# Where the first gate pair's weights are made, and in which order the products of two gate pairs run, in a hybrid attention layer

## The chip, the cores and the metric

The kernel runs on one core of one Trainium2 chip. The metric is the device time of one execution in microseconds (us). A core has five engines that work through lists of their own, each in order: TensorE (PE in the profile; PEld are its weight loads), VectorE (DVE), ScalarE (ACT), GpSimd (POOL) and SyncE (SP), whose list is here the list of DMA transfers. They wait for one another by semaphores.

## The reference

One decoder layer on 2048 tokens of width 1024: a normalised input times one combined projection, two kinds of attention, two gated branches, a merge under two sigmoid gates, an output projection and a last norm.

```python
xn = rms_norm(h, norm_gain[l])
proj = xn @ w_in[l]
sb_q, sb_k, sb_v, sw_q, sw_k, sw_v, sb_z, sw_z, g_sb, g_sw = jnp.split(proj, offsets, axis=-1)
o_sb = stick_breaking_attention(...)
...
o_sw = sliding_window_sink_attention(q, k, ...)
y_sb = (o_sb * jax.nn.silu(sb_z)) @ w_branch_sb[l]
y_sw = (o_sw * jax.nn.silu(sw_z)) @ w_branch_swa[l]
merged = jax.nn.sigmoid(g_sb) * y_sb + jax.nn.sigmoid(g_sw) * y_sw
h = h + merged @ w_out[l]
```

The columns `sb_z`, `sw_z`, `g_sb` and `g_sw` of the projection are the gates. They need nothing of the attention, so their products can stand anywhere; the change is about them.

## The kernel before

**Tiling.** Tokens are cut in four groups of 512 (`GT`), columns of the projection in tiles of 128, the inner dimension in 8 slices of 128 (`KT`). Two halves, groups 2 and 3 first (half 0), then 0 and 1 (half 1), each go through projections, sliding-window attention, stick-breaking attention and gates. Every number is split in a high and a low part, and a product of two slices is three matmuls of 128x512: high by high, high by low, low by high (L415 to L417 in `gemm`, L688 in `seven`). A column tile of one group is 24 matmuls, of both groups 48.

**Weights.** `load` (L162) fetches a raw tile of 512 KB into a ring of two buffers, `raw`. `weights` (L167) splits it: ScalarE casts the high part `wh` (L109), VectorE subtracts for the low part `wl` (L112); `wh` and `wl` are rings of three buffers each. Half 0 writes both parts to DRAM (`kept`), and half 1 loads them from there. A buffer of a ring is given out in the order of the source and becomes free when its last reader is done.

**Gate tiles alone.** `gts` are the gate tiles. In each half `gts[1]` and `gts[2]` run alone ahead of the stick-breaking stage, `gts[3:rest]` (`REST` is 12 and 18) are woven between its rows, and two more follow it.

**Gate pairs.** From `gts[rest+2]` to `gts[25]` (14 to 25 in half 0, 20 to 25 in half 1) two tiles are taken together (`gate_pair`, L721): a 2x2 block product of two tiles by two groups in seven products instead of eight (`seven`, L682), each of 4 slices, 12 matmuls. The weight operands are called `11`, `12` (tile `a`, one ring buffer `t1`), `s2`, `s3` (buffer `t3`), `s1`, `22` (buffer `t2`) and `s4`; those of the tokens `11`, `21`, `t1` to `t4`. `pair_weights` (L631) makes the weight operands on ScalarE and VectorE from the raw tiles `a` and `b`: `t1` is `a` itself, the others are sums and differences of halves of both (L656 to L661), which overwrite a part of `b`. The first pair of half 0 is made early, ahead of the stick-breaking stage, and goes to DRAM as `p0` to `p3`, each with a high and a low part. A pair that is `plain` also stores `b` as it was, for which half of it is split first, in a `tmp` called `t5`. The other five pairs of half 0 are made where they are used; the first two of these are plain like the early one, the last three also go to DRAM as `p0` to `p3`, and are the three pairs of half 1, which loads them.

**What sets the order.** TensorE's order is that of the source, by hand (`manual_schedule`). In these stages the orders of ScalarE, VectorE and SP are decided by a scheduler. `in_line` (L738) steps through the pairs: the first pair's products `11` and `12·21` (it is the `lead`), then `s2·t2`, `s1·t1`, `s3·t3`, `22·t4`, then the next pair's weights and its `11`, then the first pair's last product `s4·22`; a pair that isn't the lead has `12·21` behind `s2·t2`. `u2` and `u3` are sums out of a PSUM bank that the next product writes again (L703, L710), `use` applies the gate function and the sums of other branches and stores.

Of the kernel before, what the change touches and what calls it, by code (L numbers as in the profile page):

```python
# [17 lines left out]
P = 128  # L18
# [24 lines left out]
def f32(ap):  # L43
    return ap.bitcast(F32)
# [3 lines left out]
def tile_kernel(ctx, tc, x, xt, meta, metat, gain, w_in, w_sb, w_sw, w_out, sinks, fgain,  # L48
# [579 lines left out]
            parted("t4", k, b21)  # L628
        yield q

    def pair_weights(bp, ca, cb, plain, early=False):  # L631

        t1, t3, t2 = ([wp.tile([P, KT, P], F32R, tag=t, name=t, bufs=3) for t in ("wh", "wl")] for _ in range(3))
        if early:
            t4 = [tmp(F32R).rearrange("p (k c) -> p k c", k=KT // 2) for _ in range(2)]
        else:
            t4 = [bp.tile([P, KT // 2, P], F32R, tag=t, name=t, bufs=2) for t in ("s4h", "s4l")]
        key = w_in.name, ca, cb
        if key in kept:
            for ts, ks in zip((t1, t3, t2, t4), kept[key]):  # L640
                for t, k in zip(ts, ks):
                    DMA(t, k)
        else:
            a, b = load(ca), load(cb)
            s = tp.tile([P, KT, P], F32, tag="vt", name="s", bufs=1)
            s4 = tmp().rearrange("p (k c) -> p k c", k=KT // 2)
            lo, hi = slice(0, KT // 2), slice(KT // 2, KT)

            def parts(hl, t):
                A.copy(hl[0], t)  # L650
                V.tensor_tensor(hl[1], t, f32(hl[0]), op=ALU.subtract)
            parts(t1, a)
            if plain:
                t5 = [tmp(F32R).rearrange("p (k c) -> p k c", k=KT // 2) for _ in range(2)]
                parts(t5, b[:, lo])
            V.tensor_tensor(s[:, hi], a[:, lo], b[:, lo], op=ALU.subtract)  # L656
            V.tensor_tensor(b[:, lo], b[:, lo], b[:, hi], op=ALU.add)
            V.tensor_tensor(s[:, lo], b[:, lo], a[:, lo], op=ALU.subtract)
            parts(t3, s)
            parts(t2, b)  # L660
            V.tensor_tensor(s4, a[:, hi], s[:, lo], op=ALU.subtract)  # L661
            parts(t4, s4)
            if plain:
                for c in (ca, cb):
                    kept[w_in.name, c] = [dram(f"{e}_{w_in.name}_{c}", [P, KT, P], F32R) for e in "hl"]
                for k, t in zip(kept[w_in.name, ca], t1):
                    DMA(k, t)
                for k, t, u in zip(kept[w_in.name, cb], t5, t2):
                    DMA(k[:, lo], t)
                    DMA(k[:, hi], u[:, hi])  # L670
            if early or not plain:
                kept[key] = []
                for n, ts in enumerate((t1, t3, t2, t4)):
                    kept[key].append([dram(f"p{n}{e}_{ca}", list(t.shape), F32R) for e, t in zip("hl", ts)])
                    for k, t in zip(kept[key][n], ts):
                        DMA(k, t)
        (t1h, t1l), (t3h, t3l), (t2h, t2l) = t1, t3, t2
        lo, hi = slice(0, KT // 2), slice(KT // 2, KT)
        return {"11": (t1h[:, lo], t1l[:, lo]), "12": (t1h[:, hi], t1l[:, hi]), "s2": (t3h[:, lo], t3l[:, lo]),
                "s3": (t3h[:, hi], t3l[:, hi]), "s1": (t2h[:, lo], t2l[:, lo]), "22": (t2h[:, hi], t2l[:, hi]), "s4": t4}  # L680

    def seven(w, b, tag, use, lead):  # L682

        def product(acc, n, m, first, last):
            (wh, wl), (bh, bl) = w[n], b[m]
            for k in range(KT // 2):
                for i, (l, r) in enumerate(((wh, bh), (wh, bl), (wl, bh))):
                    T.matmul(acc, lhsT=l[:, k, :], rhs=r[:, k, :], start=first and k == i == 0,  # L688
                             stop=k == KT // 2 - 1 and i == 2, skip_group_check=not (first and last))
        a0, p1 = ps("g"), tmp()  # L690
        product(a0, "11", "11", True, lead)
        A.copy(p1, a0)
        if lead:
            a3 = ps(tag)
            product(a3, "12", "21", True, True)
            t = tmp()
            V.tensor_tensor(t, a3, p1, op=ALU.add)
            use(0, 0, t)
        yield
        a1, a2 = ps("z"), ps("t")  # L700
        u2, u3 = tmp(), tmp()
        product(a1, "s2", "t2", True, False)
        V.tensor_tensor(u2, a1, p1, op=ALU.add)  # L703
        if not lead:
            product(a0, "12", "21", False, True)
            use(0, 0, a0)
        a3 = ps(tag)
        product(a2, "s1", "t1", True, False)
        product(a1, "s3", "t3", False, True)
        V.tensor_tensor(u3, a1, p1, op=ALU.add)  # L710
        product(a3, "22", "t4", True, True)
        V.tensor_tensor(p1, a2, u3, op=ALU.add)
        V.tensor_tensor(u3, a3, u3, op=ALU.add)
        use(1, 1, p1)
        use(1, 0, u3)
        yield
        product(a2, "s4", "22", False, True)
        V.tensor_tensor(u2, a2, u2, op=ALU.add)
        use(0, 1, u2)

    def gate_pair(bp, ga, gb, groups, q, tag, plain, lead, times):  # L721
        tiles = ga, gb

        def use(m, n, t):
            c0, dst, silu, src = tiles[m]
            e = tmp()
            A.activation(e, t, AF.Sigmoid)
            if silu:
                V.tensor_tensor(e, t, e, op=ALU.mult)
            if times:  # L730
                o = ring_x()
                DMA(o, src[groups[n]])
                V.tensor_tensor(e, e, o, op=ALU.mult)
            DMA(dst[groups[n]], e)
        w = pair_weights(bp, ga[0], gb[0], plain)
        yield
        yield from seven(w, q, tag, use, lead)

    def in_line(pairs):

        for n, g in enumerate(pairs):
            if n == 0:
                next(g)
                yield n
                next(g)
            next(g)
            if n + 1 < len(pairs):
                next(pairs[n + 1])
                next(pairs[n + 1])
            drain(g)  # L750
            yield n

# [553 lines left out]
    for half, groups in enumerate(halves):  # L1306
# [42 lines left out]
        with tc.tile_pool(name=f"sb{half}", bufs=1, side="left") as bp:  # L1349
            hsplit[0] = vsplit[0] = True  # L1350
            next_sums = {g: sums() for g in halves[1]} if half == 0 else {}
            side = stick(groups, bp, [(x[g * GT + i * P:g * GT + (i + 1) * P, f * GT:(f + 1) * GT], ssq[:, f, i:i + 1])
                                      for g, ssq in next_sums.items() for i in range(4) for f in range(2)])
            drain(tiles_by_tile(gts[1:2], groups))
            rest = REST[half]
            if half == 0:
                pair_weights(None, gss[0][rest + 2][0], gss[0][rest + 3][0], True, True)
            drain(tiles_by_tile(gts[2:3], groups))
            cost_sb = 8 * sum(4 * (4 - g) for g in groups) * 1.31 + 8 * 0.75
            ratio = cost_sb / ((rest - 3) * 10.4)  # L1360
            weave(tiles_by_tile(gts[3:rest], groups), side, ratio)
            drain(side)
        with tc.tile_pool(name=f"pairs{half}", bufs=1, side="left") as bp:
            ts = [mk() for mk in gts[rest:rest + 2]]
            sums_q = sums_of_x(bp, groups)
            tq = next(sums_q)
            for n, (w, use, _) in enumerate(ts):
                for i, g in enumerate(groups):
                    drain(lagged(col_tile(w, g, use, bank="gz"[i])))
            order = gss[half]  # L1370
            todo = in_line([gate_pair(bp, order[n], order[n + 1], groups, tq, ("o", "zm")[n // 2 % 2],
                                      half == 0 and n < PLAIN, n == rest + 2, half == 0) for n in range(rest + 2, 26, 2)])
            next(todo)
            next(sums_q)
            for n in todo:
                if half == 0 and n == 4:
                    t, u = (tmp()[:, :8] for _ in range(2))
                    for n, ssq in enumerate(next_sums.values()):
                        V.tensor_tensor(t[:, 4 * n:4 * n + 4], ssq[:, 0], ssq[:, 1], op=ALU.add)
                    rs = tp.tile([P, 8], F32, tag="rs8", name="rs", bufs=1)  # L1380
                    rsqrt(rs, t, tp, t=u)
                    rs0, rs1 = rs[:, :4], rs[:, 4:]
# [71 lines left out]
```

## Time and profile before

| what | us |
|---|---|
| three runs, median | 2141.4 |
| lowest and highest of the three | 2139.36 and 2141.83 |
| the profiled execution itself | 2139.68 |
| span of the profiled execution | 2138.0 |
| TensorE busy in it | 2091.8 |
| VectorE busy | 1497.1 |
| ScalarE busy | 1079.3 |
| mean granted clock of TensorE | 0.995 |

Times in profile rows count from the start of the span. A row of the timeline gives start, length, engine, line, operation and its tiles (buffer numbers left out), and in brackets how long the engine stood idle before it and what ended that. The gate tiles alone stand in half 0 around 371 us, its pairs from 637.6 us on, the pairs of half 1 from 1612 us on.

### The profile page before, as it was taken

The numbers are of one execution on the slowest core, as the hardware profiler recorded it, in microseconds if no ns is written. First come the engines' busy times: TensorE is split into PE (matmuls) and PEld (weight loads), VectorE is DVE, ScalarE is ACT, GpSimd is POOL, SyncE is SP. The second block draws the span as 40 slices with busy tenths as digits, with TensorE's granted clock in tenths as the row PEclk, the third lists the DMA queues.
The fourth block names the chain that finished last, engine by engine and source line by source line (L and its number), as shares of the span: only waits on it lengthen the run. The fifth ranks groups of instructions, "written<-read, shape, count | busy, mean of one in ns | idle before, by whom it ended". The sixth has DMA issues, their size and how long they took to land.

```text
span 2138.0 us, 29936 instructions
## 1 busy us (share of the span) xinstructions
PE 2091.8 (98%) x10426; PEld 1736.9 (81%) x10426; DVE 1497.1 (70%) x2389; ACT 1079.3 (50%) x2442; POOL 184.1 (9%) x373
## 2 busy tenths in 40 slices
PE   8999999899998999999999999999999999999998
PEld 7788887678877888888888888888888888887887
DVE  7897885578887863777756888989996336554453
ACT  6677774566643343677754656656552312221121
POOL 2122331000000000122210000000000000000000
PEclk9999999899999999999999999999999999999999
DMA  9855544975446985444446333333226786558532
GB/s 340 301 169 191 180 166 171 348 226 176 151 147 214 339 306 177 152 147 146 154 159 186 116 107 119 124 119 108 81 89 217 263 322 197 191 204 284 156 111 79
DMA packets 181142, 397.16 MB, mean 186 GB/s; under 512 B 23456, under 2 KB 41696, under 8 KB 180992
## 3 DMA queue, kind: packets, MB, share of 16 engines
q1 hardware_dynamic: 180992, 395.26, 54.5%
q8 instruction: 82, 1.34, 0.3%
q14 instruction: 68, 0.56, 0.1%
HBM read 245.74 MB, written 149.37 MB: 185 GB/s over the span
## 4 chain that ended last, share of the span: by engine, by line
PE 82%; DVE 8%; DMA 5%; ACT 3%; issue 2%; SPq 1%; DVEq 0%; ACTq 0%
PE ps_g L415 11%; PE ps_g L417 11%; PE ps_g L416 11%; PE ps_o L1106 5%; PE ps_t L1075 5%; PE ps_z L1050 5%; PE ps_o L934 3%; PE ps_z L888 2%; PE ps_z L688 2%; PE ps_t L688 2%; PE ps_g L688 2%; PE ps_g L237 1%; PE ps_g L238 1%; PE ps_g L236 1%; PE ps_z L238 1%
## 5 line engine op out<-in xcount | busy, mean ns | idle before, releaser
L415 PE MATMUL ps_g<-xh,wh 128*128 128x512 f32 x1224 | 503.2, 411 | 19.1 <-ACT wh L109 12.3
L416 PE MATMUL ps_g<-xl,wh 128*128 128x512 f32 x1224 | 481.4, 393 | 0.0
L417 PE MATMUL ps_g<-xh,wl 128*128 128x512 f32 x1224 | 481.2, 393 | 0.0
L415 PEld LDWEIGHTS ps_g<-xh,wh 128*128 128x128 f32 x1224 | 231.8, 189 | 56.1 <-ACT wh L109 12.7
L417 PEld LDWEIGHTS ps_g<-xh,wl 128*128 128x128 f32 x1224 | 230.7, 188 | 52.6 <-DVE wl L112 0.8
L416 PEld LDWEIGHTS ps_g<-xl,wh 128*128 128x128 f32 x1224 | 232.2, 190 | 36.0 <-DVE xl L1159 1.3
L1053 ACT ACTIVATE row<-ps_z 128x512 f32<-128x512 f32 (+2 forms) x320 | 165.4, 518 | 180.0 <-PE ps_z L1050 176.5
L1062 DVE TENSOR_TENSOR_SCAN row<-row 128x528 f32<-128x528 f32 (+1 forms) x192 | 210.6, 1097 | 19.8 <-ACT row L1053 15.4
L116 DVE SCALAR_TENSOR_TENSOR wtl<-ps_t,wth 128x512 fp32r<-128x512 f32 (+1 forms) x320 | 189.7, 593 | 18.5 <-ACT wth L115 17.8
L115 ACT ACTIVATE wth<-ps_t 128x512 fp32r<-128x512 f32 (+1 forms) x320 | 170.6, 533 | 58.3 <-PE ps_t L1075 56.0
L1060 DVE TENSOR_TENSOR_SCAN row<-row,mask 128x512 f32<-128x512 f32 (+4 forms) x128 | 144.2, 1131 | 69.1 <-ACT row L1053 68.0
L1050 PE MATMUL ps_z<-kt,q 128*128 128x512 f32 (+4 forms) x640 | 178.9, 355 | 0.0
L1075 PE MATMUL ps_t<-ident,row 128*128 128x128 f32 x1088 | 171.9, 273 | 6.3 <-DVE wtl L116 3.8
L1075 PEld LDWEIGHTS ps_t<-ident,row 128*128 128x128 f32 x1088 | 134.4, 140 | 41.1 <-DVE wtl L116 6.7
L1050 PEld LDWEIGHTS ps_z<-kt,q 128*128 128x128 f32 x640 | 117.4, 188 | 22.1 <-ACT row L1053 0.4
L1106 PE MATMUL ps_o<-wth,vc 128*128 128x512 f32 (+1 forms) x320 | 130.7, 409 | 1.0 <-ACT tmp L1110 0.9
L896 ACT ACTIVATE sc<-sc,nm 128x129 f32<-128x129 f32 x256 | 100.0, 393 | 40.9 <-DVE nm L894 40.2
L1106 PE MATMUL ps_o<-wtl,vc 128*128 128x512 f32 (+1 forms) x320 | 117.1, 366 | 0.2
L112 DVE TENSOR_TENSOR wl<-raw,wh 128x1024 fp32r<-128x1024 f32 (+1 forms) x51 | 58.4, 1145 | 45.6 <-ACT wh L109 40.8
L1066 POOL COPY xs<-row 128x16 f32<-128x16 f32 x128 | 28.8, 225 | 668.8 <-DVE row L1062 590.1
L583 ACT ACTIVATE tmp<-ps_g 128x512 f32<-128x512 f32 x72 | 43.1, 598 | 65.2 <-PE ps_g L417 60.2
L301 ACT ACTIVATE sq<-res 128x512 bf16<-128x512 f32 x32 | 20.2, 632 | 109.3 <-DVE res L297 107.0
(421 smaller groups left out, 4132.5 us busy)
## 6 DMA issues: line engine op xcount, KB each, us to landing
wh<-h_in_w_in SPq DMA_DIRECT2D x60, 512.0 KB
wl<-l_in_w_in SPq DMA_DIRECT2D x60, 512.0 KB
raw<-in_w_in SPq DMA_DIRECT2D x50, 512.0 KB
h_in_w_in<-wh SPq DMA_DIRECT2D x41, 512.0 KB
l_in_w_in<-wl SPq DMA_DIRECT2D x41, 512.0 KB
q<-qd SPq DMA_DIRECT2D x128, 128.0 KB
vc<-vd SPq DMA_DIRECT2D x48, 256.0 KB
kd<-tmp SPq DMA_DIRECT2D x32, 256.0 KB
```

The lines of the kernel that those rows point to most:

```text
L115: A.activation(h, acc, AF.Copy, scale=scale)
L116: V.scalar_tensor_tensor(l, acc, scale, f32(h), op0=ALU.mult, op1=ALU.subtract)
L415: T.matmul(acc, lhsT=wh[:, k, :], rhs=xh[g][:, k, :], start=k == 0, stop=False)
L416: T.matmul(acc, lhsT=wh[:, k, :], rhs=xl[g][:, k, :], start=False, stop=False)
L417: T.matmul(acc, lhsT=wl[:, k, :], rhs=xh[g][:, k, :], start=False, stop=k == KT - 1)
L688: T.matmul(acc, lhsT=l[:, k, :], rhs=r[:, k, :], start=first and k == i == 0, stop=k == KT // 2 - 1 and i == 2, skip_group_check=not (firs ...
L1050: T.matmul(acc[:, :b - a], lhsT=lq, rhs=kt[h][:, k0 + a:k0 + b], start=t == 0, stop=t == 1)
L1053: A.activation(r[:, a:b], acc[:, :b - a], AF.Sigmoid, scale=-1.0)
L1060: V.tensor_tensor_scan(r[:, :w], r[:, :w], mask[0][:, :w], 1.0, op0=ALU.mult, op1=ALU.max)
L1062: V.tensor_tensor_scan(r[:, :w], r[:, :w], r[:, :w], last[j], op0=ALU.mult, op1=ALU.min)
L1075: T.transpose(tr[:, j * P:(j + 1) * P], rows_of[h, g, n - (j > i), j][:, k0:k0 + P], ident)
L1106: T.matmul(o[:, :n], lhsT=v, rhs=r, start=first and r is wh, stop=last and r is wl)
```

## The change

Three things are moved, and two VectorE additions come in.

1. In both halves the weights of `gts[1]` and `gts[2]` are made first, then the products of the one and of the other, and in half 0 the first pair's early weights behind both. Before, these weights stood between the two tiles.
2. `pair_weights` becomes a generator that makes `t1` first and the other operands at its second step.
3. The first two pairs are both `lead`, and `in_line` runs the first pair's `11` and `12·21`, then the second's `11` and `12·21`, then the rest of the first. The second pair's other weights are made behind the first pair's products up to `22·t4`, ahead of its last. The bank of the lead's `12·21` is always `z`.

```diff
-        if early:
+        if bp is None:
             t4 = [tmp(F32R).rearrange("p (k c) -> p k c", k=KT // 2) for _ in range(2)]
...
+        t1 = ring("11", "12")
+        key = w_in.name, ca, cb
+        old = kept.get(key)
+        if old:
+            fill(t1, old[0])
+        else:
+            a, b = load(ca), load(cb)
+            A.copy(t1[0], a)
+            V.tensor_tensor(t1[1], a, f32(t1[0]), op=ALU.subtract)
+        yield w
+        t3, t2 = ring("s2", "s3"), ring("s1", "22")
...
-            a3 = ps(tag)
+            a3 = ps("z")
             product(a3, "12", "21", True, True)
...
-        w = pair_weights(bp, ga[0], gb[0], plain)
+        ws = pair_weights(bp, ga[0], gb[0], plain)
+        w = next(ws)
         yield
-        yield from seven(w, q, tag, use, lead)
+        products = seven(w, q, tag, use, lead)
+        next(products)
+        yield
+        next(ws)
+        yield
+        yield from products
 
     def in_line(pairs):
 
+        first, second = pairs[:2]
+        for step in (first, first, first, second):
+            next(step)
+        yield 0
+        next(second)
         for n, g in enumerate(pairs):
-            if n == 0:
-                next(g)
-                yield n
-                next(g)
             next(g)
-            if n + 1 < len(pairs):
-                next(pairs[n + 1])
-                next(pairs[n + 1])
+            for more in pairs[n + 1:n + 2]:
+                if n:
+                    next(more)
+                    next(more)
+                next(more)
             drain(g)
             yield n
...
-            drain(tiles_by_tile(gts[1:2], groups))
             rest = REST[half]
+            ts = [mk() for mk in gts[1:3]]
+            for t in ts:
+                drain(by_group([t], groups))
             if half == 0:
-                pair_weights(None, gss[0][rest + 2][0], gss[0][rest + 3][0], True, True)
-            drain(tiles_by_tile(gts[2:3], groups))
+                drain(pair_weights(None, gss[0][rest + 2][0], gss[0][rest + 3][0], True))
...
-                                      half == 0 and n < PLAIN, n == rest + 2, half == 0) for n in range(rest + 2, 26, 2)])
+                                      half == 0 and n < PLAIN, n < rest + 6, half == 0) for n in range(rest + 2, 26, 2)])
```

The lists of the engines show what that moves. ScalarE in half 0 ahead of the stick-breaking stage, before: L583 are the evictions of `gts[1]` (4422, 4450) and of `gts[2]` (4544), `tmp_4469` is the cast of `t5`, the L109 rows cast `gts[2]` (4509) and `gts[3]` (4575).

```order
L583 ACTIVATE tmp_4422<-ps_g_4397 128x512
L583 ACTIVATE tmp_4450<-ps_g_4425 128x512
L650 CAST tmp_4469<-raw_4463 128x512
L650 CAST wh_4455<-s_4465 128x1024
L650 CAST wh_4457<-raw_4463 128x1024
L650 CAST tmp_4459<-tmp_4466 128x512
L109 CAST wh_4509<-raw_4511 128x1024
L583 ACTIVATE tmp_4544<-ps_g_4519 128x512
```

The same place of the change: the first two evictions are those of `gts[1]`, the next two those of `gts[2]`, and `tmp_4535` is the cast of `t5`.

```order
L583 ACTIVATE tmp_4432<-ps_g_4407 128x512
L583 ACTIVATE tmp_4460<-ps_g_4435 128x512
L583 ACTIVATE tmp_4488<-ps_g_4463 128x512
L583 ACTIVATE tmp_4516<-ps_g_4491 128x512
L668 CAST tmp_4535<-raw_4523 128x512
L1051 ACTIVATE xq_4859,ssq_4385<-xq_4859 128x512
L1051 ACTIVATE xq_4861,ssq_4385<-xq_4861 128x512
L668 CAST wh_4527<-s_4533 128x1024
```

The early pair's casts moved from behind one tile's evictions to behind those of both.

VectorE at the seam of the first and the second pair of half 0, before: L657, L658 and L661 make sums of the second pair's `a` (7636) and `b` (7638), L718 adds the first pair's last product (`ps_t_7558`).

```order
L657 TENSOR_TENSOR raw_7638<-raw_7638 128x512
L658 TENSOR_TENSOR s_7640<-raw_7638,raw_7636 128x512
L661 TENSOR_TENSOR tmp_7641<-raw_7636,s_7640 128x512
L718 TENSOR_TENSOR tmp_7559<-ps_t_7558,tmp_7559 128x512
L651 TENSOR_TENSOR wl_7631<-s_7640,wh_7630 128x1024
```

The same place of the change, where L674, L675 and L678 are those sums, L732 the addition of the last product, and L747 belongs to the gate of the product before.

```order
L747 TENSOR_TENSOR tmp_7666<-tmp_7666,xs_7669 128x512
L732 TENSOR_TENSOR tmp_7604<-ps_t_7603,tmp_7604 128x512
L674 TENSOR_TENSOR raw_7521<-raw_7521 128x512
L675 TENSOR_TENSOR s_7679<-raw_7521,raw_7519 128x512
L678 TENSOR_TENSOR tmp_7680<-raw_7519,s_7679 128x512
L669 TENSOR_TENSOR wl_7674<-s_7679,wh_7673 128x1024
```

The addition of the last product moved ahead of the three sums.

TensorE behind the first pair's `12·21` of half 1, before: `wh_17612` is that pair's `t1`, `wh_17614` its `t3`, and the rows behind the seam are its `s2·t2`.

```order
L688 MATMUL ps_o_17683<-xh_8575,wl_17613 128x512
L688 MATMUL ps_o_17683<-xh_8575,wh_17612 128x512
L688 MATMUL ps_o_17683<-xl_8576,wh_17612 128x512
L688 MATMUL ps_o_17683<-xh_8575,wl_17613 128x512
L688 MATMUL ps_z_17702<-t2h_17446,wh_17614 128x512
L688 MATMUL ps_z_17702<-t2l_17447,wh_17614 128x512
```

The same place of the change: `wh_17615` is the first pair's `t1`, `wh_17665` the second pair's, which takes the same buffer of the ring.

```order
L702 MATMUL ps_z_17634<-xh_8578,wl_17616 128x512
L702 MATMUL ps_z_17634<-xh_8578,wh_17615 128x512
L702 MATMUL ps_z_17634<-xl_8579,wh_17615 128x512
L702 MATMUL ps_z_17634<-xh_8578,wl_17616 128x512
L702 MATMUL ps_g_17709<-xh_8578,wh_17665 128x512
L702 MATMUL ps_g_17709<-xl_8579,wh_17665 128x512
```

The second pair's `11` moved from behind the first pair's `22·t4` to directly behind its `12·21`.

More of the change, by code (lines that the diff above doesn't have):

```diff
@@ L629, in sums_of_x, with pair_weights, ring, fill @@
         yield q
-    def pair_weights(bp, ca, cb, plain, early=False):
-        t1, t3, t2 = ([wp.tile([P, KT, P], F32R, tag=t, name=t, bufs=3) for t in ("wh", "wl")] for _ in range(3))
-        if early:
+    def pair_weights(bp, ca, cb, plain):
+        lo, hi = slice(0, KT // 2), slice(KT // 2, KT)
+        w = {}
+        def ring(n, n2):
+            t = [wp.tile([P, KT, P], F32R, tag=t, name=t, bufs=3) for t in ("wh", "wl")]
+            w[n], w[n2] = ([u[:, c] for u in t] for c in (lo, hi))
+            return t
+        def fill(ts, ks):
+            for t, k in zip(ts, ks):
+                DMA(t, k)
+        t1 = ring("11", "12")
[10 more added lines that the diff above has]
+        if bp is None:
             t4 = [tmp(F32R).rearrange("p (k c) -> p k c", k=KT // 2) for _ in range(2)]
@@ L637, in pair_weights @@
             t4 = [bp.tile([P, KT // 2, P], F32R, tag=t, name=t, bufs=2) for t in ("s4h", "s4l")]
[L638 to L642, printed above, removed]
+        w["s4"] = t4
+        if old:
+            for ts, ks in zip((t3, t2, t4), old[1:]):
+                fill(ts, ks)
         else:
-            a, b = load(ca), load(cb)
             s = tp.tile([P, KT, P], F32, tag="vt", name="s", bufs=1)
             s4 = tmp().rearrange("p (k c) -> p k c", k=KT // 2)
-            lo, hi = slice(0, KT // 2), slice(KT // 2, KT)
             def parts(hl, t):
@@ L651, in parts @@
                 V.tensor_tensor(hl[1], t, f32(hl[0]), op=ALU.subtract)
-            parts(t1, a)
             if plain:
@@ L670, in pair_weights @@
                     DMA(k[:, hi], u[:, hi])
-            if early or not plain:
+            if bp is None or not plain:
                 kept[key] = []
@@ L676, in pair_weights @@
                         DMA(k, t)
[L677 to L680, printed above, removed]
+        yield w
     def seven(w, b, tag, use, lead):
```

## The prediction

> **What bounds the kernel now.** I read the head of the page first, then the costliest groups, then the idle times in TensorE's timeline.
>
> ```profile
> span 2138.0 us, 29936 instructions
> PE 2091.8 (98%) x10426; PEld 1736.9 (81%) x10426; DVE 1497.1 (70%) x2389; ACT 1079.3 (50%) x2442; POOL 184.1 (9%) x373
> PE 82%; DVE 8%; DMA 5%; ACT 3%; issue 2%; SPq 1%; DVEq 0%; ACTq 0%
> L415 PE MATMUL ps_g<-xh,wh 128*128 128x512 f32 x1224 | 503.2, 411 | 19.1 <-ACT wh L109 12.3
> ```
>
> TensorE is busy for 98% of the span and is on 82% of the chain that ended last. The change adds and removes no matmul, so only two things can move the time: how long TensorE stands still (about 46 us in all), and how long it then runs at a lower clock. The last row names the largest single stop: 12.3 us, ended by ScalarE's cast at L109. These are the stops of TensorE in the places that the change touches (the bracket gives the idle time ahead of the matmul and what ended it):
>
> ```profile
> 383.79 0.80 PE L415 MATMUL ps_g<-xh,wh 128*128 128x512 f32 x1 [12.27 <-ACT wh L109]
> ...
> 652.16 0.50 PE L688 MATMUL ps_z<-t3h,wh 128*128 128x512 f32 x1 [3.52 <-DVE tmp L703]
> 665.42 0.50 PE L688 MATMUL ps_z<-t2h,wh 128*128 128x512 f32 x1 [0.50 <-ACT wh L650]
> 666.83 0.50 PE L688 MATMUL ps_z<-t2h,wl 128*128 128x512 f32 x1 [0.68 <-DVE wl L651]
> 686.23 0.50 PE L688 MATMUL ps_z<-t2h,wh 128*128 128x512 f32 x1 [0.51 <-ACT wh L650]
> 687.63 0.50 PE L688 MATMUL ps_z<-t2h,wl 128*128 128x512 f32 x1 [0.67 <-DVE wl L651]
> ...
> 1624.27 0.50 PE L688 MATMUL ps_z<-t3h,wh 128*128 128x512 f32 x1 [1.06 <-DVE tmp L703]
> ```
>
> The first stands at the gate tiles ahead of the stick-breaking stage of half 0, the next five in the pairs of half 0, the last in those of half 1. Beside the idle time there is the clock (after the comma behind the busy times: granted clock, DMA share, GB/s):
>
> ```profile
> 371.00:384.00 13.00, 0.73 (x4) 0.31 (x3) 5.96 (x8) 4.66 (x6) 0.00 (x0) 0.70 0.93 289
> 384.00:390.00 6.00, 5.96 (x14) 4.18 (x15) 1.00 (x1) 0.00 (x0) 0.00 (x0) 0.51 1.04 416
> 652.00:657.00 5.00, 4.84 (x14) 3.87 (x15) 0.91 (x3) 0.00 (x0) 0.00 (x0) 0.66 0.29 107
> 1622.00:1625.00 3.00, 1.94 (x9) 1.31 (x8) 2.81 (x5) 0.00 (x0) 0.00 (x0) 1.00 0.23 87
> ```
>
> After 12.27 us of idling the next 6.0 us run at 0.51, which costs 6.0 x 0.49 = 2.9 us; after 3.52 us the next 5.0 us run at 0.66, 1.7 us; after 1.06 us the clock stays at 1.00. So a stop of some 3.5 us pays a surcharge, one of 1 us doesn't.
>
> **The change, part by part.** All terms are against the profiled execution, 2139.68 us (span 2138.0 and 1.68 around it). It lies 1.7 us under the median of the three runs, 2141.4.
>
> *Term 1, the gate tiles of half 0.* The 12.27 us are a chain:
>
> ```profile
> 372.06 0.61 ACT L650 CAST tmp<-raw 128x512 fp32r<-128x512 f32 x1
> ...
> 374.88 0.69 DVE L661 TENSOR_TENSOR tmp<-raw,s 128x512 f32<-128x512 f32 x1
> ...
> 375.53 1.14 SPq L58 DMA_DIRECT2D q<-qd  x2
> 376.77 0.55 SPq L58 DMA_DIRECT2D raw<-in_w_in  x1
> ...
> 382.70 1.04 ACT L109 CAST wh<-raw 128x1024 fp32r<-128x1024 f32 x1 [5.31 <-DMA raw<-in_w_in]
> ```
>
> The cast of `t5` stands on ScalarE behind the eviction of the first gate tile; L661, the last reader of raw buffer `a`, ends at 375.57; then the load of the next tile's raw weights issues, lands 5.93 us later, and its cast lets TensorE go on. The change puts the second gate tile's products (48 matmuls) ahead of this work in the source. But the rows of the order show the `t5` cast, on ScalarE, behind the evictions of both tiles, with the last reader of `a` (now L678) behind it and the raw weights of the third gate tile waiting for that reader. TensorE's order is the old one: the third tile's first matmul comes before the first rows of stick-breaking attention, so nothing stands in for it. The same chain starts about 11 us later, from the end of the second tile, and stops TensorE as long, with the same 2.9 us of slow clock. The two loads of `q` that held the queue between 375.53 and 376.67 are no longer just ahead of it, up to -1.2 us; loads of keys, values and x now are, and they share DMA engines that are 93% busy. I take -0.5 us; ends: -3 (half of the landing time saved) and +3 (half as much again).
>
> *Term 2, the pairs of half 0.* Here the stops sum to 3.52+0.50+0.68+0.51+0.67 = 5.88, with the 1.7 of slow clock **7.6 us before**. For after I replay the new order with these durations:
>
> ```profile
> 637.60 0.39 PE L688 MATMUL ps_g<-xh,wh 128*128 128x512 f32 x1
> ...
> 640.32 0.39 PE L688 MATMUL ps_zm<-xh,wh 128*128 128x512 f32 x1
> ```
> ```profile
> 643.02 1.06 ACT L650 CAST wh<-raw 128x1024 fp32r<-128x1024 f32 x1 [1.91 <-PE ps_zm L688]
> ```
> ```profile
> 646.08 1.22 DVE L651 TENSOR_TENSOR wl<-raw,wh 128x1024 fp32r<-128x1024 f32 x1
> ...
> 664.28 0.69 DVE L661 TENSOR_TENSOR tmp<-raw,s 128x512 f32<-128x512 f32 x1
> 664.96 0.69 DVE L718 TENSOR_TENSOR tmp<-ps_t,tmp 128x512 f32<-128x512 f32 x1
> ```
>
> A product of 12 matmuls takes 640.32-637.60 = 2.72 us. (a) The second pair's `11` now follows the first pair's `12·21` at 643.05. Its weights take the ring buffer that this very product frees: the cast at 643.02 lasts 1.06, so TensorE waits 1.0; the low part stands on VectorE behind the added L711 and two L601 (0.6 each), at 645.05 to 646.27, so the third matmul waits 1.75. Before, four products (10.9 us) lay between. (b) The rest of the first pair: the sum `u2` ahead of the third product is due at 657.2, TensorE at 656.75: 0.45 wait, where 3.52 and the slow clock were. (c) The first pair then ends with `s4·22` at 665.35, and the second pair's `s2·t2` comes directly behind, since its `11` is spent. On VectorE the eviction of `s4·22` (L732) now stands ahead of L674 and L675, which make that operand; before, L657, L658 and L661 stood ahead of L718. So: L732 666.0 to 666.7 (behind the gating of the products before), L674 to 667.4, L675 to 668.05, ScalarE's cast to 669.1: 3.8 us of waiting, 0.75 more for the low part, and, as after 3.52, 1.7 of slow clock. (d) From the second to the third pair L674 is ahead of L732 but L675 behind it: 0.7+0.7+1.05 = 2.45 and 0.75, where 0.51+0.67 were. Later pairs keep the additions ahead of the eviction. After: 2.75+0.45+3.8+0.75+1.7+3.2 = 12.65, so **+5.0 us**. Ends: 0, if (c) and (d) hide as well as the 0.5 and 0.7 of before, and +7, if (b) keeps 2 us.
>
> [...]
>
> *Term 3, the pairs of half 1.* There the weights come ready from DRAM, in the same ring of three:
>
> ```profile
> 1617.57 0.32 SPq L58 DMA_DIRECT2D wh<-p0h  x1
> 1617.99 0.38 SPq L58 DMA_DIRECT2D wl<-p0l  x1
> ```
> ```profile
> 1618.00:1619.00 1.00, 1.00 (x6) 0.80 (x6) 0.94 (x3) 0.17 (x1) 0.00 (x0) 1.00 0.47 111
> 1619.00:1620.00 1.00, 1.00 (x6) 0.84 (x5) 1.00 (x3) 1.00 (x2) 0.00 (x0) 1.00 0.87 295
> 1620.00:1621.00 1.00, 1.00 (x6) 0.82 (x5) 1.00 (x2) 1.00 (x3) 0.00 (x0) 1.00 1.03 401
> 1621.00:1622.00 1.00, 1.00 (x6) 0.83 (x5) 1.00 (x3) 0.86 (x2) 0.00 (x0) 1.00 0.59 242
> ```
>
> The second pair's first weights are loaded when the first pair's `12·21` gives its buffer back, 1617.57. The two 512 KB pieces are 1.05 MB; the traffic of these four microseconds is 111+295+401+242 = 1049 KB, so they are in at about 1620.7 and 1621.9. Before, TensorE wanted them four products (10.9 us) later. Now the product on them is the very next: it waits 1617.5 to 1621.9, less two matmuls, **4.0 us** in two pieces of 3.2 and 0.8, too short each for the slow clock by the rows. The 1.06 us at 1624.27 (`u2` late behind other VectorE work) go. The later weights have two products, 5.4 us, ahead of them against 4.3 of loading. +2.9 us; ends: +1 (load at the peak rate of these rows), and +6.6 (a landing as slow as 5.93, and 1.7 of slow clock).
>
> Of the two added VectorE operations (0.69 each) one is counted in (a), the other lies inside the stop of term 3. GpSimd's list is unchanged. **Sum: -0.5+5.0+2.9 = +7.4**, 2147.1 from the profiled execution, 2148.8 from the median; I take 2148.
>
> **The rivals.** *The large stop really goes.* If the `t5` cast and L674 to L678 ran during the second tile's products, the raw weights would land under those 11 us: 12.3+2.9 = 15.2 us less, and with terms 2 and 3 2139.7-15.2+7.9 = 2132. It is decided by whether the cast gets ahead of the second tile's evictions on ScalarE. For it: the operands are there early. Against it: an engine works through its list in order, and the list has it behind. *The cover holds.* If in the pairs the loads and casts come as early as today, term 2 is 0 to 2 and term 3 is 1 to 2: about 2142, no difference. For it: the stops of before at these seams are only 0.5 to 0.7. Against it: the ring buffer of (a) and of term 3 can't be free sooner than the product that reads it. *Everything collides.* Upper ends together, about 2156.
>
> **How the numbers follow.** About 0.2% (4.3 us) is what a measurement of this kernel can tell from no change. The forecast has 0.60, of which 0.08 lies above 2154 with the collisions; the cover that holds 0.28; the large stop gone 0.08, with 0.04 for other gains below 2137. So slower 0.60, same 0.28, faster 0.12. From 2139 to 2154 holds some 8 in 10.
>
> **What would show it.** A stop of 11 to 13 us ahead of a first-tile cast at L109, near 395 instead of 384, shows term 1 right; none there, wrong. Stops of 1 and 1.8 us ahead of the second pair's `11`, 3 to 4 us ended by the cast of `s` ahead of its `s2·t2`, and no 3.5 us ahead of `t3`, show term 2. A stop of 3 us in half 1 ended by a load of `wh` shows term 3. A VectorE order in which the time at the pairs falls below that of before would make the prediction wrong.

## The result, and the profile after

| | median us | lowest to highest | span of the profiled execution |
|---|---|---|---|
| before, four runs | 2140.39 | 2139.36 to 2141.83 | 2138.0 |
| changed, four runs | 2156.23 | 2155.76 to 2159.17 | 2153.8 |

The changed kernel is slower: the ratio is 1.0076, with a 95% interval of 1.0059 to 1.0094. That is 15.8 us, on the side that was forecast and outside the range.

The head of the changed kernel's page and its costliest group:

```profile
span 2153.8 us, 29938 instructions
PE 2098.7 (97%) x10426; PEld 1741.7 (81%) x10426; DVE 1499.5 (70%) x2391; ACT 1079.1 (50%) x2442; POOL 182.5 (8%) x373
L415 PE MATMUL ps_g<-xh,wh 128*128 128x512 f32 x1224 | 503.0, 411 | 19.3 <-ACT wh L109 12.3
```

TensorE has as many instructions as before, yet it is busy 6.9 us longer (2098.7 against 2091.8): matmuls took longer. The other 8.9 us of the span are idle time. The stop of 12.3 us is still the largest. The stops of TensorE in the changed kernel, by its timeline:

```profile
394.40 0.80 PE L415 MATMUL ps_g<-xh,wh 128*128 128x512 f32 x1 [12.35 <-ACT wh L109]
...
426.24 1.19 PE L1073 MATMUL ps_z<-kt,q 128*128 128x512 f32 x2 [2.47 <-DMA q<-qd]
...
646.13 0.50 PE L702 MATMUL ps_g<-xh,wh 128*128 128x512 f32 x1 [0.91 <-ACT wh L651]
648.41 0.79 PE L702 MATMUL ps_g<-xh,wl 128*128 128x512 f32 x1 [1.54 <-DVE wl L652]
673.92 0.50 PE L702 MATMUL ps_z<-t2h,wh 128*128 128x512 f32 x1 [3.80 <-ACT wh L668]
675.19 0.79 PE L702 MATMUL ps_z<-t2h,wl 128*128 128x512 f32 x1 [0.53 <-DVE wl L669]
682.62 0.50 PE L702 MATMUL ps_z<-t3h,wh 128*128 128x512 f32 x1 [0.66 <-DVE tmp L717]
696.27 0.50 PE L702 MATMUL ps_z<-t2h,wh 128*128 128x512 f32 x1 [2.46 <-ACT wh L668]
697.53 0.50 PE L702 MATMUL ps_z<-t2h,wl 128*128 128x512 f32 x1 [0.53 <-DVE wl L669]
...
1631.30 0.76 PE L702 MATMUL ps_g<-xh,wh 128*128 128x512 f32 x1 [3.67 <-DMA wh<-p0h]
```

The large stop came 10.6 us later with the same length. The 3.52 us ahead of `t3` in half 0 went (0.66 is left at the second pair), and so did the 1.06 us of half 1. In their place stand four stops at the seams of the pairs. What followed them is in the windows of the changed kernel (granted clock, DMA share and GB/s are the last three columns):

```profile
425.00:430.00 5.00, 3.76 (x13) 3.15 (x14) 1.23 (x1) 1.84 (x4) 0.00 (x0) 0.66 0.82 271
648.00:653.00 5.00, 4.59 (x11) 3.63 (x12) 5.00 (x9) 0.00 (x0) 0.00 (x0) 0.50 0.32 123
653.00:656.00 3.00, 3.00 (x12) 2.38 (x11) 3.00 (x6) 2.78 (x5) 0.00 (x0) 0.76 0.50 178
675.00:681.00 6.00, 5.81 (x19) 4.66 (x20) 4.29 (x6) 1.91 (x3) 0.00 (x0) 0.72 0.88 301
696.00:700.00 4.00, 3.20 (x13) 2.35 (x14) 3.75 (x5) 2.21 (x4) 0.00 (x0) 1.00 0.72 239
1631.00:1637.00 6.00, 5.71 (x13) 4.05 (x14) 6.00 (x11) 1.82 (x3) 0.00 (x0) 0.50 0.20 78
```

A busy count of 11 or 13 matmuls in 5 or 6 us at a clock of 0.50 is the sign: TensorE looks busy and does about half the work (its matmuls start 0.42 or 0.43 us apart from 649.00 us on, and 0.22 or 0.23 apart ahead of the stop). To see where the time came in, I cut each profiled execution at four matmuls that all kernels have: the first and the last start of a pair's product in either half. The stage lengths come from these starts in TensorE's timeline.

| kernel | start to first pair | pairs, half 0 | pairs, half 1 |
|---|---|---|---|
| before | 637.6 | 122.9 | 58.3 |
| changed | 639.6 | 130.8 | 63.9 |
| difference | +2.0 | +7.9 | +5.7 |
| forecast | -0.5 | +5.0 | +2.9 |

The three add up to 15.6 of the 15.8 us between the spans.

### The profile page after: what moved, and what is told of

Read it like the earlier page. It is cut to its first block, busy times and chain, and to the rows that moved or that the text cites. A ratio compares the mean times of both kernels' runs of the same rounds, so it can differ in the third digit from the quotient of the medians.

```text
span 2153.8 us, 29938 instructions
## 1 busy us (share of the span) xinstructions
PE 2098.7 (97%) x10426; PEld 1741.7 (81%) x10426; DVE 1499.5 (70%) x2391; ACT 1079.1 (50%) x2442; POOL 182.5 (8%) x373
## 4 chain that ended last, share of the span: by engine, by line
PE 88%; DMA 5%; DVE 3%; ACT 2%; issue 1%; SPq 1%; ACTq 0%; DVEq 0%
PE ps_g L415 12%; PE ps_g L416 12%; PE ps_g L417 12%; PE ps_o L1129 5%; PE ps_t L1098 5%; PE ps_z L1073 5%; PE ps_z L702 3%; PE ps_z L911 3%; PE ps_o L957 3%; PE ps_t L702 2%; PE ps_g L702 2%; PE ps_g L237 1%; PE ps_g L238 1%; PE ps_g L236 1%; PE ps_z L236 1%; PE ps_z L238 1%
## 5 line engine op out<-in xcount | busy, mean ns | idle before, releaser
L415 PE MATMUL ps_g<-xh,wh 128*128 128x512 f32 x1224 | 503.0, 411 | 19.3 <-ACT wh L109 12.3
L112 DVE TENSOR_TENSOR wl<-raw,wh 128x1024 fp32r<-128x1024 f32 (+1 forms) x51 | 58.3, 1143 | 34.6 <-ACT wh L109 29.8
L583 ACT ACTIVATE tmp<-ps_g 128x512 f32<-128x512 f32 x72 | 43.0, 598 | 65.5 <-PE ps_g L417 57.7
L911 PEld LDWEIGHTS ps_z<-kk,q 128*128 128x128 f32 x512 | 69.8, 190 | 6.5 <-DVE q L892 0.7
## 6 DMA issues: line engine op xcount, KB each, us to landing
q<-qd SPq DMA_DIRECT2D x128, 128.0 KB
```

The costliest lines, as they stand in the source:

```text
L415: T.matmul(acc, lhsT=wh[:, k, :], rhs=xh[g][:, k, :], start=k == 0, stop=False)
```

## The experiments

Theory: the stops were forecast rightly, and what was missed is the clock behind some of them and a collision at the start of the stick-breaking stage. Rivals are named with each run. Before was measured beside them, at 2140.84 us for the first four, 2142.67 for the next four and 2140.40 for the last four, so that runs of different fours are best compared by their difference to it. The last three columns are stage lengths in the one profiled execution of each.

| run | median us | ratio to before, 95% interval | start | half 0 | half 1 |
|---|---|---|---|---|---|
| e1_start | 2143.78 | 1.0014 (1.0004 to 1.0023) | 640.6 | 124.3 | 58.4 |
| e2_pairs | 2153.15 | 1.0056 (1.0040 to 1.0071) | 636.9 | 131.0 | 62.5 |
| e3_fill1 | 2152.82 | 1.0058 (1.0041 to 1.0076) | 641.7 | 129.4 | 61.5 |
| e4_ahead | 2130.35 | 0.9948 (0.9932 to 0.9965) | 627.6 | 122.9 | 58.4 |
| e5_own | 2151.93 | 1.0050 (1.0031 to 1.0070) | 640.1 | 129.9 | 58.6 |
| e6_order | 2142.73 | 1.0006 (0.9997 to 1.0015) | 641.1 | 121.5 | 58.5 |
| e7_fill | 2151.55 | 1.0047 (1.0030 to 1.0064) | 642.6 | 128.0 | 61.4 |
| e8_best | 2128.90 | 0.9944 (0.9924 to 0.9964) | 625.9 | 123.0 | 58.6 |
| e9_start_nw | 2136.33 | 0.9984 (0.9975 to 0.9993) | 633.5 | 123.6 | 58.4 |
| e10_before_nw | 2137.03 | 0.9983 (0.9974 to 0.9992) | 634.3 | 123.2 | 58.3 |
| e11_hold | 2154.20 | 1.0068 (1.0047 to 1.0090) | 640.4 | 126.8 | 62.6 |
| e12_best_fill | 2129.36 | 0.9947 (0.9935 to 0.9960) | 627.4 | 122.4 | 58.6 |

**Which part costs.** The new start alone, on before:

```diff
-            drain(tiles_by_tile(gts[1:2], groups))
             rest = REST[half]
+            ts = [mk() for mk in gts[1:3]]
+            for t in ts:
+                drain(by_group([t], groups))
             if half == 0:
                 pair_weights(None, gss[0][rest + 2][0], gss[0][rest + 3][0], True, True)
-            drain(tiles_by_tile(gts[2:3], groups))
```

> Before with the first part of the change alone (weights of both gate tiles first, then both tiles' products, then the early pair). Theory: the 12.3 us stop moves behind the second tile and keeps its length; with the stop of 2.5 us on a load of q that the changed kernel shows at 426 us, about +2 us: 2142. Rival: the moved work is what disturbs everything behind it, and most of the 16 us come with it: 2150 or more. If the start had only been moved without any cost: 2140.

And the opposite, the changed kernel with these lines as they were:

> The changed kernel with the start of before (the early pair's weights between the two gate tiles); the order of the pairs stays changed. Theory: some 14 us of the 16 lie in the pairs, 8 in half 0 and 5.6 in half 1: 2154. Rival (the start costs most): 2146 or less.

The start gave +2.9 us where some +2 was expected, the pairs without it +12.3: the two sum to 15.2, and the rival that puts most on the start falls. In e1_start the stop of 12.20 us stands at 394.52, and one on a load of `q` at 426.94.

**Is it the clock?** Matmuls into a spare bank whose result nothing reads (called filler below), 16 of them in the stop of half 1, where three pairs run, and none in half 0:

```diff
+    FILL = {3: 16, 6: 0}
+
+    def fill(n):
+        if n:
+            acc = ps("t")
+            for i in range(n):
+                T.matmul(acc, lhsT=xh[0][:, i % KT, :P], rhs=xh[0][:, i % KT, :], start=i == 0, stop=i == n - 1)
...
         yield 0
+        fill(FILL[len(pairs)])
         next(second)
```

> The changed kernel with 16 matmuls into an unused PSUM bank put behind the second plain product of the first pair in half 1, where TensorE stands still for 3.67 us; nothing reads them. Theory: the stop itself stays (its load is no earlier), but TensorE is busy in it, so the clock isn't lowered behind it: 6 us at 0.50 are won back, -3 us: 2153. Rival: the matmuls behind the stop are slow for another reason (loads landing late, PSUM): no gain, 2156; if the filler reaches past the stop, up to +1.

It won 3.4 us against the changed kernel. The stage of half 1, the only one that the edit touches, shrank by 2.4, from 63.9 to 61.5. TensorE's timeline and a window of e3_fill1, at the place that had 3.67 us and a clock of 0.50:

```profile
1633.06 0.50 PE L702 MATMUL ps_g<-xh,wl 128*128 128x512 f32 x1 [0.48 <-DMA wl<-p0l]
```
```profile
1632.00:1638.00 6.00, 5.51 (x24) 4.23 (x25) 6.00 (x11) 2.33 (x5) 0.00 (x0) 1.00 0.14 54
```

The load is no earlier; the filler fills the wait, 24 matmuls instead of 13 fit in the six microseconds behind it, and the clock is 1.00. So the surcharge is the clock's.

Fillers of 11, 16 and 11 matmuls in the stops of half 0 as well:

> The changed kernel with matmuls that nothing reads in four stops: 11 ahead of the second pair's 11 in half 0, 16 and 11 behind the last products of its first and second pair, 16 in half 1. Theory: the stops stay as long as they are, the slow clock behind them goes, 3.2 and 1.8 us in half 0 and 3.4 in half 1: 2148. Rival (the surcharge of half 0 isn't the clock, or the fillers are longer than the stops): 2152 or more.

The windows of e7_fill at the two slow places of half 0:

```profile
648.00:653.00 5.00, 4.75 (x21) 3.64 (x20) 4.74 (x7) 1.61 (x2) 0.00 (x0) 1.00 0.52 205
675.00:681.00 6.00, 5.47 (x23) 4.05 (x22) 4.61 (x6) 2.45 (x4) 0.00 (x0) 1.00 0.86 276
```

The clock stays at 1.00, and half 0 takes 128.0 us in place of 130.8, half 1 61.4. The sum over the whole kernel is a miss: 2151.55 and not 2148. A part of it is the measure: before stood at 2142.67 beside this run, and the distance to it is 8.9 us, where 2148 lies 7.6 above the 2140.39 beside the changed kernel. Two more reasons can be read in the stages: the start took 642.6 us in this execution, 3 more than in the changed kernel, with a first stop of 13.16 us; and half 0 was already between 129.4 and 131.0 in e2_pairs, e3_fill1 and e5_own, whose pairs there are those of the changed kernel, so its surcharge isn't 5 us in each run.

**Is the ring buffer the whole of the stop in half 1?** `own` is set for the second pair of half 1 alone:

```diff
-        t1 = ring("11", "12")
+        if own:
+            t1 = [wp.tile([P, KT, P], F32R, tag="raw", name="own", bufs=2) for _ in "hl"]
+            w["11"], w["12"] = ([u[:, c] for u in t1] for c in (lo, hi))
+        else:
+            t1 = ring("11", "12")
...
```

> The changed kernel, but in half 1 the second pair's first weights go to the two raw buffers, which are free there, and not to the ring buffer that the first pair's product 12·21 must give back. Theory: the ring buffer alone makes the load late; the stop of 3.67 us in half 1 goes, with its 3 us of slow clock, and nothing comes for it: 2149 to 2150. Rival: the late load is one of several things that stand there (PSUM bank z shared, VectorE behind), and a stop of over 1 us is left: 2152 or more.

The stop on the load went; half 1 is 58.6 us, 5.3 less. One of 1.41 us came for it, in e5_own's timeline:

```profile
1639.44 0.50 PE L706 MATMUL ps_z<-t3h,wh 128*128 128x512 f32 x1 [1.41 <-DVE tmp L721]
```

That is the old wait for `u2`, 1.06 before: VectorE's additions are late again as soon as TensorE isn't. Even with free buffers the changed order of half 1 wins nothing on before (58.6 against 58.3). So the buffer was the whole of that stop, but not all that stands there: the rival's stop of over 1 us came. The time, 2151.93, lies above the stated 2149 to 2150 mostly because before was slower beside it: the distance to before is 9.3 us, and 2149 to 2150 was 8.6 to 9.6 above the 2140.39.

**Is it the order or the second lead?**

```diff
         w = next(ws)
-        yield
-        products = seven(w, q, tag, use, lead)
-        next(products)
-        yield
         next(ws)
         yield
-        yield from products
+        yield from seven(w, q, tag, use, lead)
...
```

with `in_line` as before, so that the second pair's weights, `11` and `12·21` come behind the first pair's `22·t4`.

> The changed kernel with the order of the pairs undone: the second pair's weights whole and behind the first pair's product 22·t4, then its 11 and 12·21, then the first pair's last product. It keeps the new start and the second pair as a lead. Theory: what costs in the pairs is the place of the second pair's products ahead of its weights, not that it is a lead; left are the 2 to 3 us of the start, and the seam of 0.5 and 0.7 us is covered by one product more: 2142 to 2144. Rival: the additional eviction of the lead on VectorE costs as well: 2147 or more.

It is the order: 2142.73 beside a before of 2142.67, and half 0 is 1.4 us shorter than before, since the seam of 0.50 and 0.68 us is covered. The lead's extra additions cost nothing that shows.

**Is the stop of 3.8 us spent cover?** In half 0 the second pair yields between its `11` and its `12·21`:

```diff
+        if lead > 1:
+            yield
         if lead:
             a3 = ps("z")
             product(a3, "12", "21", True, True)
...
-        yield
+        if lead < 2:
+            yield
...
```

> The changed kernel, but in half 0 the second pair's product 12·21 is kept back until behind the first pair's last product, ahead of its own s2·t2. Theory: the stop of 3.8 us there is cover that the change spent; 2.7 us of cover back leave some 1.1 and 0.5 us, too short for the slow clock: -4.5 us, 2151 to 2153. Rival: VectorE's order sets the stop and moves along with the product: 2156.

The timeline and a window of e11_hold at that seam:

```profile
669.86 0.50 PE L702 MATMUL ps_z<-t2h,wh 128*128 128x512 f32 x1 [1.09 <-ACT wh L668]
671.20 0.50 PE L702 MATMUL ps_z<-t2h,wl 128*128 128x512 f32 x1 [0.61 <-DVE wl L669]
```
```profile
671.00:677.00 6.00, 5.80 (x18) 4.62 (x19) 6.00 (x9) 2.38 (x4) 0.00 (x0) 0.72 0.89 322
```

3.80 became 1.09: one product of 2.7 us is what was missing. The half shrank by 4.0 us, of which the shorter stop is 2.6 (1.09+0.61 for 3.80+0.53); the rest is slow clock that came behind other stops than in the changed kernel. For the clock went to 0.72 behind 1.09+0.61 us all the same, which the expectation held to be too short. One of its four executions took 5280.23 us, which nothing here explains; the median of the other three, 2154.20, is 2.0 us better than the changed kernel and misses the stated range.

**What the +2 us of the start are.** The stores of `p1` to `p3` are left out in both, whose values are therefore not those of the reference:

```diff
                 for n, ts in enumerate((t1, t3, t2, t4)):
+                    if early and n:
+                        first = kept[key][0]
+                        kept[key].append(first if n < 3 else [k[:, :KT // 2] for k in first])
+                        continue
```

> e1_start without the stores of p1 to p3 of the early pair (2.6 MB, some 6.5 us of the DMA engines at 400 GB/s); the first pair later reads p0 in their place, so its values are not the reference's, and its loads are as many. Theory: the 2 to 3 us of the moved start are loads of q that queue behind these stores, since the stick-breaking stage now begins in the middle of them; without the stores the stop of 2 to 4 us on q near 427 us goes, and the time lies within 1 us of e10_before_nw. Rival: the start costs for another reason, and 2 to 3 us stay between the two.

> Before, without the same stores, as the measure for e9_start_nw. Theory: here the stores run under the second gate tile's products; the stop at 384 us gets shorter by what the raw load no longer shares, 0 to 3 us: 2137 to 2141. Rival: no stop at all is left, 2126.

2136.33 against 2137.03: the moved start costs nothing when the stores are gone. (The 400 GB/s of the estimate are near what before moves in single windows: 416 from 384 to 390 us, 412 from 415 to 420.) A window of e1_start, and the same of e9_start_nw:

```profile
425.00:430.00 5.00, 3.01 (x12) 2.29 (x12) 1.50 (x2) 1.68 (x6) 0.00 (x0) 0.83 0.94 309
```
```profile
425.00:430.00 5.00, 5.00 (x28) 4.12 (x27) 3.30 (x4) 3.26 (x6) 0.00 (x0) 1.00 1.00 298
```

With the stores TensorE idles 2 of the 5 us at a lower clock; without them it is busy throughout, and its timeline has no stop on `q`. The large stop didn't shrink in either (12.37 and 13.31): these stores aren't what makes it long. So the 2137.03 of e10_before_nw lies in the stated range for another reason than the stated one; two stops of 0.85 and 1.64 us near 440 us, which before has, are gone in it.

**Can the large stop go?** Before, with the third tile's weights ahead of the early pair:

```diff
-            drain(tiles_by_tile(gts[1:2], groups))
             rest = REST[half]
             if half == 0:
+                ts = [mk() for mk in gts[1:4]]
+                for t in ts[:2]:
+                    drain(by_group([t], groups))
                 pair_weights(None, gss[0][rest + 2][0], gss[0][rest + 3][0], True, True)
-            drain(tiles_by_tile(gts[2:3], groups))
+                woven = chain(by_group(ts[2:], groups), tiles_by_tile(gts[4:rest], groups))
...
```

> Before, with the weights of three gate tiles made ahead of the early pair in half 0 (the third's raw load no longer waits for the pair's raw buffer), products of two tiles, early pair, then the third woven as before. Theory: the stop of 12.3 us was that raw buffer alone; it goes, with its 2 to 3 us of slow clock: 2125 to 2128. Rival: the next tile's raw load waits in the same place and the stop only moves: 2137 to 2141.

10.5 us faster than before. The start is 10.0 us shorter; the rest of the 12.27 us is found in e4_ahead's timeline:

```profile
409.10 0.50 PE L415 MATMUL ps_g<-xh,wh 128*128 128x512 f32 x1 [3.07 <-ACT wh L109]
410.36 0.52 PE L417 MATMUL ps_g<-xh,wl 128*128 128x512 f32 x1 [0.53 <-DVE wl L112]
```

The next tile's raw load waits now, but most of its wait lies under the first rows of stick-breaking attention. So the stop was the raw buffer, as the chain said, and 2130.35 lies 2 us above my 2125 to 2128 and 7 below the rival's 2137 to 2141.

**A version that beats both:**

> A version meant to beat both: three gate tiles' weights ahead of the early pair as in e4_ahead, the pairs of half 0 in the order of before, those of half 1 in the changed order with the second pair's first weights in the raw buffers. Theory: e4_ahead less the 1.1 us that half 1 waits for u2 in before: 2129. Rival: the changed order costs in half 1 even with its weights there: 2132 or more.

2128.90, 0.9944 of before (0.9924 to 0.9964). It can't be told from e4_ahead. The stated 2129 was hit, but not by the stated reason: its half 1 gained nothing (58.6), and the start is 1.7 us shorter than in e4_ahead in the profiled execution. The last run put 15 filler matmuls into the 3.5 us ahead of `s3·t3`:

> e8_best with 15 matmuls that nothing reads in the stop of 3.5 us ahead of the first pair's product s3·t3 in half 0. Theory: 8 matmuls at half the clock are won back, -1.5 us against e8_best: 2127 to 2128. Rival: the clock drop there is made up elsewhere: 2129.

No gain: the stage is 122.4 against 123.0. Behind the filler a wait of 1.17 us is left, so filler and wait take 4.6 us where the stop alone was 3.5; that eats most of the 1.5 us that were expected of the clock. VectorE's timeline in e12_best_fill shows why the wait ends later:

```profile
635.12 0.69 DVE L715 TENSOR_TENSOR tmp<-ps_z,tmp 128x512 f32<-128x512 f32 x1 [0.97 <-DMA gw<-tmp]
```

VectorE stood idle for 0.97 us until a store out of a `tmp` buffer had landed, and did everything behind it later by that, `u2` too. In e8_best the same addition has no wait. The filler starts at 638.29, behind this, so in this execution it isn't the filler that made the wait longer.

## Why the prediction was wrong

**Side and stops were right.** The large stop was said to move and keep its length: 12.35 at 394.40. The second pair's `11` was to wait 1.0 and 1.75 us: it waited 0.91 and 1.54. Its `s2·t2` 3.8 and 0.75: 3.80 and 0.53. The third pair's 2.45 and 0.75: 2.46 and 0.53. Half 1 was to wait 4.0 us on a ring buffer: 3.67. The order of the lists, replayed with durations from the trace, gave each of these to within half a microsecond.

**The failed step is the clock term.** The prediction let only stops of some 3.5 us pay. In term 3 it called the wait "too short each for the slow clock by the rows", having split it into 3.2 and 0.8 us. The rows of before have 1.00 behind 1.06 us and 0.66 behind 3.52, and no run shows that 3.2 us is too short. The wait came as one stop of 3.67, and 6.0 us at 0.50 followed, a loss of 3.0 us; the term was 2.8 short. In term 2, (a) had no surcharge: 0.91+1.54 us with two matmuls between were followed by 5.0 us at 0.50 and 3.0 at 0.76, 2.5+0.7 = 3.2 us, against 2.9 missing there. (e5_own runs the same products without a slow stretch, and its first pair's `s2·t2` starts 2.8 us earlier in the half.) e3_fill1 and e7_fill show that it is the clock, since the same waits with TensorE busy have 1.00 behind them.

The clock did not fall behind the same wait in every run. The stop of 0.91+1.54 us was followed by at least six matmuls at 0.43 us from start to start, where 0.23 is usual, in the changed kernel, e2_pairs and e3_fill1, and by none in e5_own and e11_hold; that of 2.46+0.53 us by six in e2_pairs, e5_own and e11_hold, by none in the changed kernel and e3_fill1. Behind longer stops in the pairs such stretches stand too, with matmuls at 0.42 or 0.43 us from start to start: from three (e11_hold, 3.70 us) to ten (changed, 3.67), and numbers between behind the stops of before (3.52), of the changed kernel in half 0 (3.80) and of e10_before_nw (3.85).

The windows below, of 3.41 us side by side, show three of these places: two around the waits of 0.91+1.54 us and three around those of 2.46+0.53 us of the changed kernel, and two around those of 2.46+0.53 us in e2_pairs. The first time behind the comma is TensorE's busy time, the last column but two the clock.

```profile
644.21:647.63 3.42, 1.74 (x7) 0.81 (x5) 2.30 (x4) 1.65 (x2) 0.00 (x0) 1.00 0.55 213
647.63:651.04 3.41, 2.63 (x6) 2.15 (x7) 3.41 (x6) 0.00 (x0) 0.00 (x0) 0.50 0.55 219
692.00:695.41 3.41, 1.81 (x8) 1.15 (x7) 2.91 (x5) 0.53 (x2) 0.00 (x0) 1.00 0.97 312
695.41:698.82 3.41, 2.02 (x8) 1.37 (x9) 3.02 (x4) 2.80 (x4) 0.00 (x0) 1.00 0.58 183
698.82:702.24 3.42, 3.42 (x17) 2.83 (x16) 2.20 (x4) 0.00 (x0) 0.00 (x0) 1.00 0.90 286
```
```profile
689.90:693.31 3.41, 0.73 (x2) 0.30 (x2) 2.99 (x5) 2.28 (x3) 0.00 (x0) 1.00 0.71 220
693.31:696.72 3.41, 3.34 (x8) 2.66 (x9) 2.96 (x5) 0.75 (x2) 0.00 (x0) 0.50 0.90 305
```

In the changed kernel the wait of 2.46+0.53 us is shared by two of these windows, which have 1.60 and 1.39 us without work, and the clock stays at 1.00; in e2_pairs 2.68 us without work lie in one, and the next has 0.50. Ahead of the 0.50 at 647.63 stand 1.68 us. These are three places; what decides between 1.00 and 0.50, they don't show.

The size of the miss varies with this. Behind the stop of half 1 ten matmuls at 0.42 or 0.43 us from start to start came in the changed kernel (3.67 us) and three in e11_hold (3.70 us), whose half 1 took 62.6 us and not 63.9; in e2_pairs it took 62.5.

**Term 1 had the wrong sign.** -0.5 was taken, with +3 as its end, and +2.0 came. The chain was right; the step that failed is the assumption that nothing behind it would change. The stick-breaking stage starts in the middle of the early pair's stores, the loads of `q` come late for it (2.47 us and 0.66 of the clock behind them), and e9_start_nw against e10_before_nw shows that the stores are the cause.

**The rivals.** The cover did not hold, and the large stop did not go. "Everything collides", put at 2156 with a chance of 0.08, gave the right time, but mostly by luck. Its +3 at the start was a slower landing of the raw weights, and that stop stayed as it was; its +7 in half 0 was a wait at (b), and none over 0.4 us is left there; of its +6.6 in half 1 the slow clock came, and the slow landing did not.

## What to carry to other kernels

Running a product early spends it: it no longer covers the making of the weights behind it, and it needs its own buffer before the ring has given one back. Before reordering, ask of each operand which reader frees its buffer and how many products then stand between; a product directly behind that reader waits for the whole load or cast (here 3.67 us for the load of half 1, and 0.91 and 1.54 us for the cast and the low part of half 0). And look at waits of TensorE that stand close together as one, and at the clock behind them: here 1.00 stood behind 1.06 us alone, 0.50 behind 0.91+1.54 us in the changed kernel and 1.00 or 0.50 behind 2.46+0.53 us, in the changed kernel and in e2_pairs. The price of a slow stretch in these pairs is an estimate from the windows, their length times the missing share of the clock: 1.7 us behind the 3.52 us of before (5.0 us at 0.66), 3.0 behind the 3.67 us of the changed kernel (6.0 us at 0.50), 3.2 behind its 0.91+1.54 us.

## What the runs showed that I had not expected

The clock fell behind waits of 1.09 and 0.61 us (0.72 over the 6 us from 671 in e11_hold); behind 1.06 and 0.72 us at the same seam of e9_start_nw it stayed at 1.00. With filler matmuls the clock was 1.00 behind the stop of half 1 in e3_fill1 and behind two stops of half 0 in e7_fill, and 2.4 us of half 1 were won so in e3_fill1. And giving a stage free buffers in half 1 brought the old wait for `u2` back, at 1.41 us in place of 1.06.
